# A hybrid decoder step: halved and woven products in the state-space stage, splits held behind its recurrences, later stores and delayed cache products

## The chip, the cores and the metric

The kernel runs on one core of a Trainium2 chip. The metric is the device time of one execution in microseconds, lower is better; the time before is the median of three runs.

## The reference

Two layers, D = 1024, 576 positions: a prompt of 512 and eight samples of 8. The first layer is attention over three groups of windows and dilations with a key/value cache, the second a diagonal complex state-space layer; a SwiGLU FFN (width 2816) follows each. Everything is fp32. The state-space layer, where most of the change lies:

```python
u = (h @ w_in).astype(f32)
abar = jnp.exp(lam * dt)                     # lam: complex, 64 groups x 64 states
bbar = ((abar - 1.0) / lam)[..., None] * bmat
# in chunks of time, state carried from one to the next:
bu = jnp.einsum('gpc,btgc->btgp', bbar, uk)
a_cum, x0 = lax.associative_scan(combine, (a_el, bu), axis=1)
xs = x0 + a_cum * hc[:, None]
y = jnp.einsum('gcp,btgp->btgc', cmat, xs).real   # + d_skip * u
g = jax.nn.gelu(y)
z = g @ w_glu
val, gate = jnp.split(z, 2, axis=-1)
return val * jax.nn.sigmoid(gate), h_last
```

The outputs are both results, the three shifted caches for prompt and samples, and the new states.

## The kernel before

Every large product is made of three: the weights and the activations are each split into a high part, rounded to the fp32r type, and a low rest, and high·high, low·high and high·low are summed in a PSUM bank. ScalarE makes the high part of a weight tile (`whi`, line 99) and VectorE the rest (`wlo`, line 100); `mm6` (line 108) issues the six products of a tile of 128 x 128 weights (two halves of 288 positions). Weights come in tiles of 512 KB on SP's DMA queue. `pace(rate)` adds the rate to a credit at each weight load and sends one store of the shifted cache (`o_kv_s`, line 83, about 1 MB) for each full unit; RF is the usual rate.

The stages follow each other: QKV projection in 36 steps j with the attention of cached samples woven in; attention of the prompt; output projection; FFN 0; the state-space layer; FFN 1. Instructions are put on each engine's queue by a scheduler that follows the order in which the code issues them and reorders what is ready.

In the QKV steps, `begin` handles the group of the longest cache: the tiles `kc` (keys) and `qb` (queries) are loaded one step ahead, and VectorE multiplies and reduces them (`P<-kc`). The list `due` holds the pairs of this step; `later(n, fn)` runs `fn` n slots on. VectorE also makes the norms of the projected rows (the five `sh<-t` reduces of a chunk), which the scores wait for. `kc` and `qb` share six buffers.

`ssm_setup` builds the constants of the state-space layer as a generator during FFN 0: after each half of a projection there, `fill` runs it to its next `yield`. We call this a tick. It makes E (powers of abar, on POOL), then for each of eight blocks f the matrices W, T and V, and stores all in DRAM. T comes from VectorE, V from POOL.

`ssm_phase` treats the width of 1024 as eight blocks f of 128 channels. `stage1(c)` projects two blocks (u = h w_in), stores the rows of u and loads them back in the layout of U. `stage2(f)` multiplies U by W into a PSUM bank (line 1423, 128 x 64 pieces), copies it to Sb (line 1425, ScalarE) and runs the recurrence over chunks on VectorE (lines 1438 to 1451): rotate by E, scan, rotate back, write Xt. `stage3(f)` adds T·U and V·Xt (lines 1461 and 1462), applies gelu (1464), stores the rows of y and loads them back, and splits them (lines 173 and 174) for the last product. `consts(f, q)` loads W, E, T and V of a block on queue q: blocks 0 to 3 during FFN 0, and block f + 4 behind `stage3(f)` on ScalarE's queue. There are three banks `acc` and one double bank `aux`. `glu_first` makes the first column of the GLU product: two banks for the gate (`pg`), two for the value (`pv`), over two halves of the contraction, rows of y 0 to 3 and 4 to 7.

## Time and profile before

| | us |
|---|---|
| median of 3 runs (1497.78 to 1498.53) | 1497.95 |
| profiled execution | 1499.43 |
| its span | 1497.7 |
| TensorE busy in the span | 1472.2 |
| VectorE busy | 895.8 |
| ScalarE busy | 527.8 |
| POOL busy | 323.1 |

A span is from the first to the last instruction; the profiled execution's time has 1.73 us around it. The granted TensorE clock was 0.998. A row of the timeline is start, duration, engine, line, operation, output<-input, tile form and shape, count, and in brackets the idle time of the engine before it with what released it. A row of the waits is engine, line, releaser: total, times, longest. A row of a stretch is its bounds and length, then busy time and instructions of PE, PE's weight loads, VectorE, ScalarE and POOL, then clock, DMA share and GB/s. A row of a DMA issue ends with KB and the median time to landing. SPq, ACTq and POOLq are the DMA queues of the engines.

### The profile page before, as it was taken

The page shows a single profiled execution, that of the slowest core. Times are in us where ns is not written, and L with a number is a line of the kernel's source. Part 1 is how long each engine was busy: PE and PEld are TensorE (multiplying, and loading weights), DVE is VectorE, ACT ScalarE, POOL GpSimd, SP SyncE. Part 2 cuts the span into 40 slices and gives each one's busy share as a digit, 9 for nine tenths or more (in the row PEclk, how much of TensorE's full clock was granted, in tenths as well). Part 3 has the DMA queues.
Part 4 walks back from the last instruction along what each step waited for, and adds up shares of the span by engine and source line. Part 5 has one row for each costly group of instructions (what it writes and reads, how often), then busy time and mean ns, then how long its engine had stood idle before and what let it go on. Part 6 is the DMA issues. An engine that isn't in the chain of part 4 may idle for free. (4 is left out here: it accounts for less than half of the span.)

```text
span 1497.7 us, 29564 instructions
## 1 busy us (share of the span) xinstructions
PE 1472.2 (98%) x12406; PEld 1384.5 (92%) x12406; DVE 895.8 (60%) x1507; ACT 527.8 (35%) x814; POOL 323.1 (22%) x377
## 2 busy tenths in 40 slices
PE   9999999999999999999999999999999999999998
PEld 7888777777899999999999999899999999999998
DVE  5898988745569545388687768745443323333332
ACT  4534455465552211322223453433432212221222
POOL 2022231320030174134436520201111001100100
PEclk9999999999999999999999999999999999999999
DMA  7566788989875555677867668865555655442212
GB/s 248 209 234 229 237 278 270 365 295 348 247 252 191 204 212 204 245 238 282 288 203 246 221 219 262 232 217 168 186 197 196 223 195 195 137 138 85 83 56 81
DMA packets 191861, 322.64 MB, mean 215 GB/s; under 512 B 40016, under 2 KB 138128, under 8 KB 190320
## 3 DMA queue, kind: packets, MB, share of 16 engines
q1 hardware_dynamic: 183488, 303.24, 60.0%
q10 hardware_dynamic: 5072, 10.04, 2.0%
q0 software_dynamic: 3168, 7.48, 1.5%
q8 instruction: 97, 1.59, 0.4%
q14 instruction: 36, 0.29, 0.1%
HBM read 289.22 MB, written 118.78 MB: 272 GB/s over the span
## 5 line engine op out<-in xcount | busy, mean ns | idle before, releaser
L108 PE MATMUL acc<-xgh,wlo 128*128 128x288 f32 x1760 | 377.9, 296 | 2.2 <-DVE wlo L100 2.2
L108 PE MATMUL acc<-xgh,whi 128*128 128x288 f32 x1760 | 379.1, 297 | 0.1
L108 PE MATMUL acc<-xgl,whi 128*128 128x288 f32 x1760 | 377.7, 296 | 1.0 <-DVE xgl L174 1.0
L100 DVE TENSOR_TENSOR wlo<-raw,whi 128x1024 fp32r<-128x1024 f32 (+1 forms) x166 | 214.9, 1295 | 261.9 <-ACT whi L99 258.4
L99 ACT ACTIVATE whi<-raw 128x1024 fp32r<-128x1024 f32 (+1 forms) x166 | 172.4, 1038 | 476.2 <-PE acc L108 446.0
L108 PEld LDWEIGHTS acc<-xgh,wlo 128*128 128x128 f32 x1760 | 283.2, 188 | 2.7 <-DVE wlo L100 2.5
L108 PEld LDWEIGHTS acc<-xgl,whi 128*128 128x128 f32 x1760 | 283.1, 189 | 1.5 <-DVE xgl L174 1.3
L108 PEld LDWEIGHTS acc<-xgh,whi 128*128 128x128 f32 x1760 | 282.7, 189 | 1.5 <-issue 1.0
L1029 POOL TENSOR_TENSOR gt<-gt,rstd 128x576 f32<-128x576 f32 x44 | 72.9, 1659 | 489.3 <-ACT gt L1028 489.1
L108 PE MATMUL acc<-hh,wlo 128*128 128x288 f32 x704 | 150.8, 295 | 2.1 <-DVE wlo L100 2.1
L108 PE MATMUL acc<-hh,whi 128*128 128x288 f32 x704 | 151.6, 296 | 0.0
L108 PE MATMUL acc<-hl,whi 128*128 128x288 f32 x704 | 150.9, 295 | 0.0
L340 PE MATMUL acc<-whi,xh 128*128 128x512 f32 x288 | 118.8, 414 | 0.5 <-ACT xh L280 0.4
L108 PEld LDWEIGHTS acc<-hh,wlo 128*128 128x128 f32 x704 | 112.9, 188 | 2.3 <-DVE wlo L100 2.3
L108 PEld LDWEIGHTS acc<-hh,whi 128*128 128x128 f32 x704 | 113.0, 188 | 0.6 <-issue 0.6
L108 PEld LDWEIGHTS acc<-hl,whi 128*128 128x128 f32 x704 | 113.1, 188 | 0.0
L340 PE MATMUL acc<-wlo,xh 128*128 128x512 f32 x288 | 112.2, 391 | 0.0
L340 PE MATMUL acc<-whi,xl 128*128 128x512 f32 x288 | 111.5, 393 | 0.0
L1050 DVE TENSOR_TENSOR xT<-acc,xT 128x576 f32<-128x576 f32 x48 | 36.1, 756 | 53.5 <-PE acc L108 53.5
L194 POOL TENSOR_TENSOR ssum<-ssum,sq 128x576 f32<-128x576 f32 x21 | 36.8, 1753 | 136.2 <-ACT sq L193 106.9
L340 PEld LDWEIGHTS acc<-whi,xl 128*128 128x128 f32 x288 | 54.0, 188 | 12.0
L340 PEld LDWEIGHTS acc<-whi,xh 128*128 128x128 f32 x288 | 54.0, 188 | 11.2 <-ACT xh L280 0.9
(395 smaller groups left out, 2008.5 us busy)
## 6 DMA issues: line engine op xcount, KB each, us to landing
o_kv_s<-cache_kv_w SPq DMA_DIRECT2D x64, 1020.0 KB, 6.9
kc<-cache_kv_w SPq DMA_DIRECT2D x100, 512.0 KB, 7.4
raw<-ffn_w_gate SPq DMA_DIRECT2D x44, 512.0 KB, 3.9
raw<-ffn_w_up SPq DMA_DIRECT2D x44, 512.0 KB, 3.9
raw<-ffn_w_down SPq DMA_DIRECT2D x40, 512.0 KB, 3.5
raw<-w_qkv SPq DMA_DIRECT2D x36, 512.0 KB, 7.4
kc<-qscr SPq DMA_DIRECT2D x32, 512.0 KB, 6.7
o_kv_s<-cache_kv_w SPq DMA_DIRECT2D x16, 1008.0 KB, 6.4
```

The costliest lines, as they stand in the source:

```text
L99: s.activation(hi, raw, AF.Copy)
L100: mark[0] = v.tensor_tensor(lo, raw, hi.bitcast(F32), OP.subtract)
L108: pem[0] = te.matmul(ps[:, c, :HN], w, x[:, c * HN:(c + 1) * HN], start=first and i == 0, stop=last and i == 2)
L194: g.tensor_tensor(self.ss, self.ss, sq, OP.add)
L340: ins = nc.tensor.matmul(*a, **kw)
L1029: g.tensor_tensor(t, t, nin.r, OP.mult)
L1050: v.tensor_tensor(xv, ps[m][:, :, :HN], xv, OP.add)
```

## The change

*State-space stage.* Each T and V product becomes two of 64 output columns. `stage1` takes a function `mid` that it runs inside its products: `stage2(1)` now stands before the last quarter of `stage1(2)`, `stage2(3)` and `stage3(0)` between the halves of `stage1(3)`. Constants of the second four blocks are loaded on POOL's queue: W and E behind `stage2(f)`, T and V behind `stage3(f)`. U has eight buffers, and the rows of y that come back use them too; u has two buffers of its own. The W products of blocks from 4 on alternate between two banks; Y of blocks 6 and 7 both use `aux`. The rows of y are split in two groups of four by `gsplit`, which holds the first group's splits behind Sb(7) on ScalarE and behind Xt(6) on VectorE, the second's behind the gelu of block 7 and Xt(7). `glu_first` puts `stage3(6)` and `stage3(7)` between its products and takes the second half of the contraction row by row.

*Setup.* Five yields fewer while E is made and two more between E's last copy and its store, so that what follows comes three ticks earlier; V's stores come one tick behind V's products.

*QKV steps.* In steps 8, 20, 24 and 28 the products of the cache are issued five slots later, and the closing of a sample 12 slots later instead of 10.

*Stores.* RF is 0.72 for 0.70, and the GLU weight loads send none (0.58 before).

```diff
-RF = 0.7
+RF = 0.72
...
+    def products(j, due):
+        for b, part, kc, qb in due:
+            if part == 0:
+                prods[b] = dk.tile([128, 4, 4, 8], F32, name="P2")
+                g.memset(prods[b], 0.0)
+            v.tensor_tensor(kc, kc, qb, OP.mult)
+            v.tensor_reduce(prods[b][:, :, 0:2, 2 * part:2 * part + 2].rearrange("p a h c -> p c a h"), kc.rearrange("p c (a h d) -> p c a h d", a=4, h=2),
+                            AX.X, OP.add)
+            if part == 3:
+                c = Close2(nc, L, v, s, dk, psd, "Sd", prods.pop(b), b)
+                later(12 if j <= 31 else 6, lambda c=c: close(c))
...
+        if due:
+            if j % 4 == 0 and j < 32 and CHUNKS[j // 4 - 1][0] < 2:
+                later(5, lambda: products(j, due))
+            else:
+                products(j, due)
...
-    def consts(f, q):
+    def consts_in(f, q):
         kc = kp[f // 2 % 2]
         Wc = kc.tile([128, 2, 4, 128], F32, name="Wc")
         q.dma_start(Wc, scn["W"][f])
         Ec = kc.tile([128, 2, 4, 64], F32, name="Ec")
         q.dma_start(Ec, scn["E"][f])
+        KC[f] = [Wc, Ec]
+
+    def consts_out(f, q):
+        kc = kp[f // 2 % 2]
         Tc = kc.tile([128, 8, 128], F32, name="Tc")
         q.dma_start(Tc, scn["T"][f])
         Vc = kc.tile([128, 4, 2, 128], F32, name="Vc")
         q.dma_start(Vc, scn["V"][f].rearrange("r p q l c -> (r p) q l c"))
-        KC[f] = (Wc, Vc, Tc, Ec)
-
-    out.update(Ar=Ar, Ai=Ai, E63=E63, rho=rho, x0=x0, xs0=xs0, KC=KC, consts=consts)
+        KC[f] += [Tc, Vc]
...
                 yield
-                yield
+                if k == 5:
+                    yield
             yield
             g.tensor_copy(E63, ee[:, :, :, 63])
+            yield
+            yield
             nc.sync.dma_start(scn["E"].rearrange("f p r q c -> p r f q c"), ee.rearrange("p r (f q) c -> p r f q c", f=8))
...
                 g.tensor_tensor(vv[:, 1], vv[:, 1], vt_, OP.subtract)
+                yield
                 for gl in range(2):
                     for ri in range(2):
                         nc.sync.dma_start(scn["V"][f, ri, :, :, gl, :], vv[gl * 64:gl * 64 + 64, ri].rearrange("p q c t -> p q (c t)"))
-                yield
...
+    pend, last = [], {}
+
+    def gsplit(n, a, b):
+        for f, yt in [pend.pop(0) for _ in range(n)]:
+            hi = xg.tile([128, NT], F32R, name="xgh")
+            lo = xg.tile([128, NT], F32R, name="xgl")
+            with tc.issue_after(last[a].ins):
+                s.activation(hi, yt, AF.Copy)
+            with tc.issue_after(last[b].ins):
+                v.tensor_tensor(lo, yt, hi.bitcast(F32), OP.subtract)
+            G[f] = hi, lo
...
-    def stage1(c):
+    def stage1(c, mid=None, at=(1, 0)):
...
             for m in range(2):
+                if mid and (kh, m) == at:
+                    mid()
...
-            u = wk.tile([128, 2, HN], F32, name="uP")
+            u = wk.tile([128, 2, HN], F32, name="yt", bufs=2)
...
-            U = wk.tile([128, 8, 72], F32, name="U", bufs=6)
+            U = wk.tile([128, 8, 72], F32, name="U", bufs=8)
...
-        S = acc(2)
+        S = acc(1 + f % 2 if f > 3 else 2 if f else 1)
...
         X[f] = Xt
+        if f < 4:
+            consts_in(f + 4, g)
...
-        Y = acc(0) if f % 2 else aux.tile([128, 2, 512], F32, name="aux")
+        U, (Tc, Vc) = Uc[f], KC[f][2:]
+        Y = acc(0) if f in (1, 3, 5) else aux.tile([128, 2, 512], F32, name="aux")
         for gl in range(2):
             for q in range(4):
-                o = Y[:, gl, q * 72:q * 72 + 72]
-                te.matmul(o, Tc[:, 2 * q + gl, :], U[:, 2 * q + gl, :], start=True, stop=False)
-                te.matmul(o, Vc[:, q, gl, :], X[f][:, gl, q, :], start=False, stop=True)
+                for w, x, st in ((Tc[:, 2 * q + gl, :], U[:, 2 * q + gl, :], True), (Vc[:, q, gl, :], X[f][:, gl, q, :], False)):
+                    for h in range(0, 128, 64):
+                        te.matmul(Y[h:h + 64, gl, q * 72:q * 72 + 72], w[:, h:h + 64], x, start=st, stop=not st)
...
-        yt = wk.tile([128, NT], F32, name="yt")
+        yt = wk.tile([128, 8, 72], F32, name="U", bufs=8).rearrange("p a b -> p (a b)")
         nc.sync.dma_start(yt, scn["Y"][f])
         if f < 4:
-            consts(f + 4, s)
-        G[f] = L["split"](xg, yt, None, "xgh", "xgl")
+            consts_out(f + 4, g)
+        pend.append((f, yt))
...
-        W2[c0] = [fetch_w(A["ssm_w_glu"], 2 * D, kh * 4, 4, c0, 256, 0.0 if c0 in (0, D) else 0.58) for kh in range(2)]
+        W2[c0] = [fetch_w(A["ssm_w_glu"], 2 * D, kh * 4, 4, c0, 256, 0.0) for kh in range(2)]
...
     stage2(0)
-    stage2(1)
-    stage1(2)
+    stage1(2, lambda: stage2(1), (1, 1))
     stage2(2)
-    stage2(3)
     fetch2(D)
-    stage1(3)
-    stage3(0)
+    stage1(3, lambda: (stage2(3), stage3(0)))
     stage3(1)
+    stage2(4)
     fetch2(0)
-    stage2(4)
+    stage3(2)
     stage2(5)
-    stage3(2)
     stage3(3)
     stage2(6)
     stage3(4)
     stage2(7)
-    for f in range(5, 8):
-        stage3(f)
-    sp["es"].close()
-    nout = L["Norm"](3, L["es"].enter_context(L["right"]("xg2", bufs=8)))
+    stage3(5)
+    gsplit(4, ("Sb", 7), ("Xt", 6))
...
     def glu_first():
-        pg, pv = [acc(1), acc(2)], [acc(0), aux.tile([128, 2, 512], F32, name="aux")]
-        for kh in range(2):
-            for ps, c0 in ((pg, D), (pv, 0)):
-                glu_half(ps, *split_w(W2[c0][kh]), kh)
+        pg = [acc(1), acc(2)]
+        glu_half(pg, *split_w(W2[D][0]), 0)
+        stage3(6)
+        wh, wl = split_w(W2[0][0])
+        pv = []
+        for m in range(2):
+            pv.append(aux.tile([128, 2, 512], F32, name="aux") if m else acc(0))
+            for k in range(4):
+                mm6(pv[m], wh[:, k, m * 128:(m + 1) * 128], wl[:, k, m * 128:(m + 1) * 128], *G[k], k == 0, False)
+            if m == 0:
+                stage3(7)
+        gsplit(4, ("ys", 7), ("Xt", 7))
+        sp["es"].close()
+        N[0] = L["Norm"](3, L["es"].enter_context(L["right"]("xg2", bufs=8)))
+        w = [(ps, *split_w(W2[c0][1])) for ps, c0 in ((pg, D), (pv, 0))]
+        for k in range(4):
+            for ps, wh, wl in w:
+                for m in range(2):
+                    mm6(ps[m], wh[:, k, m * 128:(m + 1) * 128], wl[:, k, m * 128:(m + 1) * 128], *G[4 + k], False, k == 3)
         return pg, pv
```

The order on TensorE around block 0 of stage 3 (L108 are products of the input projection of the last two blocks). Before, at the end of that projection:

```order
L108 MATMUL acc_10837<-xgh,whi 128x288 x2
L108 MATMUL acc_10837<-xgl,whi 128x288 x2
L108 MATMUL acc_10837<-xgh,wlo 128x288 x2
L1461 MATMUL aux<-U,Tc 128x72
L1462 MATMUL aux<-Xt,Vc 128x72
```

After, between its halves:

```order
L108 MATMUL acc_10806<-xgh,whi 128x288 x2
L108 MATMUL acc_10806<-xgl,whi 128x288 x2
L108 MATMUL acc_10806<-xgh,wlo 128x288 x2
L1454 MATMUL acc_10863<-U,Wc 64x72 x16
L1495 MATMUL aux<-U,Tc 64x72 x2
L1495 MATMUL aux<-Xt,Vc 64x72 x2
```

Block 0 now stands half a projection earlier, with the W products of block 3 (L1454) ahead of it, and T and V (both L1495) come in pairs of halves of 64 columns.

The order on VectorE at the end of the recurrences: the splits of the rows of y are L174 before and L1417 after. Before, block 7 from its first sums to its end:

```order
L1440 TENSOR_TENSOR R<-R,ta 128x256
L1441 TENSOR_TENSOR R<-R,ta 128x256
L174 TENSOR_TENSOR xgl<-yt,xgh 128x576
L1443 SCALAR_TENSOR_TENSOR Z<-tb,R 128x256 x2
L1446 TENSOR_TENSOR R<-Ec,Z 128x8x63
L1447 TENSOR_TENSOR ta<-Ec,Z 128x8x63
L174 TENSOR_TENSOR xgl<-yt,xgh 128x576
L1450 TENSOR_TENSOR Xt<-R,ta 64x4x63
L1451 TENSOR_TENSOR Xt<-R,ta 64x4x63
L1450 TENSOR_TENSOR Xt<-R,ta 64x4x63
L1451 TENSOR_TENSOR Xt<-R,ta 64x4x63
L174 TENSOR_TENSOR xgl<-yt,xgh 128x576 x4
```

After, from the end of block 6's recurrence (its last rows L1481 and L1482):

```order
L1481 TENSOR_TENSOR Xt<-R,ta 64x4x63
L1482 TENSOR_TENSOR Xt<-R,ta 64x4x63
L1417 TENSOR_TENSOR xgl<-U,xgh 128x576 x2
L1469 TENSOR_TENSOR R<-Ec,Sb 128x512
L1470 TENSOR_TENSOR ta<-Ec,Sb 128x512
L1417 TENSOR_TENSOR xgl<-U,xgh 128x576
L1471 TENSOR_TENSOR R<-R,ta 128x256
L1472 TENSOR_TENSOR R<-R,ta 128x256
L1474 SCALAR_TENSOR_TENSOR Z<-tb,R 128x256 x2
L1477 TENSOR_TENSOR R<-Ec,Z 128x8x63
L1478 TENSOR_TENSOR ta<-Ec,Z 128x8x63
L1417 TENSOR_TENSOR xgl<-U,xgh 128x576
```

The rows of y that were split inside the recurrences as they came now stand behind Xt of block 6, two of them ahead of block 7 and two inside it.

The order on VectorE in QKV step 24, where a product of the cache (`kc<-kc`, with its reduce `P<-kc`) meets the norm's reduces (`sh<-t`; `Sall` belongs to the scores). Before:

```order
L760 TENSOR_TENSOR wlo<-raw,whi 128x1024
L760 TENSOR_TENSOR kc<-kc 128x1024
L760 TENSOR_REDUCE P_1726<-kc 128x2x4x2
L760 TENSOR_REDUCE sh<-t_1887 128x8
L760 TENSOR_REDUCE sh<-t_1903 128x8
L760 TENSOR_REDUCE sh<-t_1928 128x8
L760 TENSOR_REDUCE sh<-t_1944 128x8
L760 ISA Sall,mx_77<-Sall,md 128x136
L760 ISA mx_77 128x1
L760 TENSOR_REDUCE sh<-t_1965 64x8
L760 TENSOR_TENSOR wlo<-raw,whi 128x1024
```

After:

```order
L767 TENSOR_TENSOR wlo<-raw,whi 128x1024
L767 TENSOR_REDUCE sh<-t_1885 128x8
L767 TENSOR_REDUCE sh<-t_1901 128x8
L767 TENSOR_REDUCE sh<-t_1926 128x8
L767 TENSOR_REDUCE sh<-t_1942 128x8
L767 ISA Sall,mx_77<-Sall,md 128x136
L767 ISA mx_77 128x1
L767 TENSOR_REDUCE sh<-t_1963 64x8
L767 TENSOR_TENSOR kc<-kc 128x1024
L767 TENSOR_REDUCE P_1726<-kc 128x2x4x2
L767 TENSOR_TENSOR wlo<-raw,whi 128x1024
```

The product and its reduce moved from ahead of the five reduces to behind them.

32 lines of the change are left out of this document (13 added, 19 removed).

## The prediction

> **What bounds the kernel now.** I read the page's engine table first, then the waits of TensorE, then busy time by stretch, and last the timeline of each engine where TensorE waits.
>
> ```profile
> PE 1472.2 (98%) x12406; PEld 1384.5 (92%) x12406; DVE 895.8 (60%) x1507; ACT 527.8 (35%) x814; POOL 323.1 (22%) x377
> PE acc L108 <- DVE wlo L100: 4.3, 2, 2.2
> PE Sd L578 <- ACT ks L760: 2.2, 2, 1.6
> 896.74:990.63 93.89, 90.67 (x895) 88.36 (x894) 70.64 (x119) 39.18 (x87) 11.27 (x19) 1.00 0.81 246
> ```
>
> TensorE is busy for 98% of the span, so a change can win in two ways only: less matrix work, or one of the short waits gone (engine line, releaser, us in total, times, longest). The last row is the state-space stage from the end of its second input projection to the end of the first output product: 93.89 us, of which TensorE is idle 3.2. Yet VectorE has a hole of 6.5 us in that stage:
>
> ```profile
> 905.12 0.69 DVE L1438 TENSOR_TENSOR R<-Ec,Sb 128x512 f32<-128x512 f32 x1
> ...
> 939.10 0.69 DVE L1438 TENSOR_TENSOR R<-Ec,Sb 128x512 f32<-128x512 f32 x1 [6.49 <-ACT Sb L1425]
> ...
> 945.60 0.69 DVE L1438 TENSOR_TENSOR R<-Ec,Sb 128x512 f32<-128x512 f32 x1
> ...
> 952.71 0.75 DVE L174 TENSOR_TENSOR xgl<-yt,xgh 128x576 fp32r<-128x576 f32 x1
> ...
> 958.79 0.42 DVE L1451 TENSOR_TENSOR Xt<-R,ta 64x252 f32<-64x252 f32 x1
> ```
>
> A recurrence (L1438 to L1451) takes 6.50 us (939.10 to 945.60). The fifth, of block 4, waits for ScalarE's Sb copy; the seventh has a split of a row of y inside it and ends at 959.21. The last GLU products follow that chain.
>
> ```profile
> 936.54 0.65 ACT L1464 ACTIVATE ys<-acc 128x576 f32<-128x576 f32 x1 [3.23 <-DMA u_scr<-uP]
> 938.44 0.63 ACT L1425 ACTIVATE Sb<-acc 128x576 f32<-128x576 f32 x1
> 925.03 0.57 SPq L83 DMA_DIRECT2D o_kv_s<-cache_kv_w  x1
> 926.44 2.18 SPq L1409 DMA_DIRECT2D u_scr<-uP  x2
> 936.11 0.37 SPq L1413 DMA_DIRECT2D U<-u_scr  x1
> 990.63 0.42 PE L108 MATMUL acc<-xgh,whi 128*128 128x288 f32 x2
> ```
>
> ScalarE came to the Sb copy late, behind the second gelu, which was itself held for 3.23 us, and SP sent a 1 MB cache store just ahead of the rows of u, whose loads left 9.7 us after the stores. The first product of the next GLU column starts at 990.63: the stage's end.
>
> **Halved T and V products.** Now and after:
>
> ```profile
> 930.69 0.39 PE L1461 MATMUL acc<-U,Tc 128*128 128x72 f32 x2
> ...
> 934.04 0.39 PE L1462 MATMUL acc<-Xt,Vc 128*128 128x72 f32 x2
> 934.35 1.22 PE L1423 MATMUL acc<-U,Wc 128*64 128x72 f32 x32
> 935.50 0.44 PE L1461 MATMUL aux<-U,Tc 128*128 128x72 f32 x2
> ```
>
> One block's T and V products are 32 records of 128*128, in 16 rows of two; the last starts 15 rows after the first (930.69 to 934.04), 0.223 us each, so a block takes 3.57 us. The W products already have the form that the change gives them, 128*64 with 72 columns: 32 records from 934.35 to 935.50, 1.15 us. The change makes 64 such records of a block, 2.30 us. It saves 1.27 us a block, 10.2 us over eight. Going from one form to the other costs 0.31 − 0.22 = 0.09 us (934.04 to 934.35, against 0.22 between like rows); the finer weave adds some six such borders, 0.6 us. [...] The W row bears out 3.57 / 2.30 = 1.55x, and I take that.
>
> **The weave.** I rebuild the stage from 896.74, the start of the stretch above, where both kernels start block 0's W products, with 0.1325 us for a projection product (four from 926.37 to 926.90):
>
> ```profile
> 926.37 0.42 PE L108 MATMUL acc<-xgh,whi 128*128 128x288 f32 x2
> 926.63 0.43 PE L108 MATMUL acc<-xgl,whi 128*128 128x288 f32 x2
> 926.90 0.42 PE L108 MATMUL acc<-xgh,wlo 128*128 128x288 f32 x2
> 909.44 0.73 DVE L1408 TENSOR_TENSOR uP<-acc,rs_m 128x576 f32<-128x576 f32 x1
> 581.87 1.23 DVE L100 TENSOR_TENSOR wlo<-raw,whi 128x1024 fp32r<-128x1024 f32 x1
> ```
>
> TensorE up to block 4's W products: 192 projection products (25.4), five W groups (5.8), blocks 0 and 1 of stage 3 (4.6), a wait for u of block 6 that clears the bank (some 1.3) and borders (0.3): 896.74 + 37.4 = 934.15; with ScalarE's 0.65 the fifth recurrence can start at 934.9. VectorE: block 1's W products now stand three quarters into the third projection and end near 908.6, so its recurrence starts at 909.4 instead of 905.12, a cost of 4.3 us that the old hole pays for. From there three recurrences (19.5), four rows of u (3.0), two weight splits (2.4) end at 934.3. The two engines meet within a microsecond: block 4 starts at 934.95, 4.15 earlier than 939.10. Blocks 4, 5 and 6 run without a split inside: 934.95 + 19.5 = 954.4 for the end of Xt(6), against 959.21. Behind it VectorE does two splits, block 7 and two more splits: 954.4 + 1.4 + 6.5 + 1.4 = 963.7.
>
> TensorE waits for that end, since V(6) needs it. What then follows without a break: stage 3 of block 6 (2.2), 72 products (9.5), stage 3 of block 7 (2.3, at 966.1, its Xt ready at 963.7), the gelu that clears the one aux bank (0.9), 120 products (15.9), borders (0.5): 31.3 us, ending at 985.7. Before, 990.63 − 959.21 = 31.4. So this stage gains 4.9 us: of 10.2 us of matrix work, half goes into new waits of TensorE for Xt(5) and Xt(6), some 3 us each, in place of the old ones.
>
> What hides the moved loads. The constants go to POOL's queue, in order behind waits for the recurrences; T and V of block 4 leave once block 2's recurrence is done (near 925) and are used at 941.5.
>
> ```profile
> Tc<-t_scr ACTq DMA_DIRECT2D x4, 512.0 KB, 6.4
> o_kv_p<-vt POOLq DMA_DIRECT2D x8, 256.0 KB, 6.8
> ```
>
> Landing in 6 to 7 us leaves several to spare; later blocks too. The rows of u of block 6 leave at 931.4, without the cache store; even at the old 9.7 us plus landing, W(6) at 947 just makes the recurrence at 947.95. The held splits: the last row of y is stored at 969 and needed after 980. I put all of this at nothing; without the cover it is the second rival.
>
> **First FFN, setup in fewer ticks.**
>
> ```profile
> 850.95 0.53 PE L108 MATMUL acc<-hh,wlo 128*128 128x288 f32 x2 [2.10 <-DVE wlo L100]
> 848.47 2.43 DVE L100 TENSOR_TENSOR wlo<-raw,whi 128x1024 fp32r<-128x1024 f32 x1
> 847.34 2.48 POOL L194 TENSOR_TENSOR ssum<-ssum,sq 128x576 f32<-128x576 f32 x1
> 596.56 0.53 PE L108 MATMUL acc<-xgh,wlo 128*128 128x288 f32 x2 [2.24 <-DVE wlo L100]
> 587.72 0.31 DVE L1298 MEMSET cb<- 128x128 f32 x2 [4.62 <-DMA e_scr<-ee]
> ```
>
> At 848.47 a weight split takes 2.43 us instead of 1.23 beside POOL, which is doing the last V products and sums of the norm together. Three ticks fewer put the V products before the down projection, so I count this wait gone: −2.1 (0 if the sums alone slow VectorE). [...] At 587.72 VectorE stood behind the E table's store; the store now leaves two ticks after its copy. Between 0 and −2.2, and a setup that has moved by three ticks against the gate loop can meet a weight split anew, +1 to +2: I take −1.
>
> **Delayed products of the cache.**
>
> ```profile
> 194.24 1.23 DVE L760 TENSOR_TENSOR kc<-kc 128x1024 f32<-128x1024 f32 x1 [3.53 <-DMA kc<-qscr]
> 195.50 1.22 DVE L760 TENSOR_REDUCE P<-kc 128x16 f32<-128x1024 f32 x1
> 198.51 0.43 PE L578 MATMUL Sd<-ks,Qz 128*32 128x128 f32 x8 [1.63 <-ACT ks L760]
> PE pt L566 <- DMA kc<-cache_kv_w: 1.3, 1, 1.3
> ```
>
> The 2.2 us at L578 are two waits, this one and a like one of 0.57, the rest of the sum. The norm's reduces, whose results the scores wait for, were queued behind a product that waits for its DMA; product and reduce are 2.45 us, more than either wait, and now stand behind them. −2.2 then; but the buffers come free later, and a cache tile late as in the last row costs 1.3 each, at most two: +2.6 less 2.2. I take −1.
>
> **The rest.** The store pace only moves transfers; FFN 2's tail of stores still ends ahead of the last products. Zero.
>
> **Sum.** −4.9 − 2.1 − 1 − 1 = −9.0 on the profiled 1499.43 (span 1497.7 and 1.73 around it), 1490.4; the median of the runs is 1.48 below the profiled one, so **1489.0**. No change means within 0.2%, 3.0 us.
>
> **The rivals.** *The recurrences do not hold TensorE.* Then all 10.2 us and the 3.2 idle go, less 0.6 of borders: −12.8 in the stage, 1481.1. For it: VectorE is busy only 70.64 of 93.89. Against: four recurrences in a row are 26 us and cannot start before block 4's W products. 0.10.
> *The hole stays.* Rows of u or Sb(4) come late again, block 4 starts near 939 and the end of Xt(6) at 959: the stage gains nothing, the rest −4.1, 1493.9; with the FFN and cache terms failing too, 1498. For it: block 1 starts 4.3 us later, and POOL holds the loads in order. 0.20.
> *Constants one at a time, slower.* If POOL's eight T and V transfers from 925.7 are served one after another, at 5.0 us each Vc(7) lands at 966, just in time; at 7.5 at 985.7, 19.7 late, and the stage ends at 1005.4, +14.8: 1508.6 with the other terms. Slower than before from 6.2 us each on (9 us late). For it: 6.4 to 6.8 us a landing above, with 0.81 of the DMA engines busy over the stage (its row, the number before the last). Against: median landings of loads that may have overlapped say nothing of one-at-a-time service. 0.07. [...]
> *The products stay one behind another.* If halves did not overlap, a block would take 64 records of 0.11, 7.1 us, and lose; the W row excludes it.
>
> **How the numbers follow.** Forecast 0.58 (1486 to 1493), the hole 0.20, free recurrences 0.10, slow constants 0.07, else 0.05. The range 1482 to 1497.5 takes in the first, most of the hole and half of the free case. Faster 0.80 (0.58 + 0.10 + half of the hole + 0.02), same 0.12, slower 0.08.
>
> **What would show it.** T and V rows of 128*64 with 2.3 us a block; VectorE from 909 to 934 without a hole; block 4 at 935; Xt(6) at 954; TensorE idle about 3 us before V(5) and V(6); no 2.10 wait near 850 and no 1.63 near 198. I am wrong if block 4 starts after 938, or a wait for Tc, Vc or Ec by DMA shows.

## The result and the profile after

The changed kernel takes 1489.44 us (median of 5, 1488.16 to 1493.70), the kernel before 1498.53 (median of 5) on the same chip: a ratio of 0.9938, 95% interval 0.9922 to 0.9955. One of the five runs of before stands apart at 1752.71; the others lie from 1497.78 to 1499.42. The profiled execution took 1488.62 with a span of 1486.7, so the profiled time of after is 10.8 us below that of before, and its span 11.0. The forecast was 1489.0. The sum came out; its terms did not, and the experiments are about them.

First the page's engine line and TensorE's own waits after the change (us in total, times, longest):

```profile
PE 1457.7 (98%) x12662; PEld 1370.9 (92%) x12662; DVE 896.0 (60%) x1507; ACT 526.8 (35%) x814; POOL 335.4 (23%) x393
...
PE acc L1454 <- DMA U<-u_scr: 9.3, 1, 9.3
...
PE acc L108 <- DVE wlo L100: 1.9, 2, 1.7
...
PE pt L573 <- DMA kc<-cache_kv_w: 1.4, 2, 1.1
```

TensorE is busy 14.5 us less (1472.2 to 1457.7) and the weight splits cost it 1.9 instead of 4.3. The 2.2 us of the scores are gone. In their place stands one wait of 9.3 us that the prediction did not have: the W products of a block (L1454) for the rows of u.

To see where the 11.0 us come from, compare the same landmarks in both timelines of TensorE: the first scores of the prompt, the first product of FFN 0, block 0's W products. Before:

```profile
304.78 0.66 PE L760 MATMUL S<-kT,att 64*32 64x256 f32 x16
424.14 0.42 PE L108 MATMUL acc<-xgh,whi 128*128 128x288 f32 x2
896.74 1.22 PE L1423 MATMUL acc<-U,Wc 128*64 128x72 f32 x32
```

After, with the first product of the next GLU column, which ends the stage:

```profile
301.29 0.66 PE L767 MATMUL S<-kT,att 64*32 64x256 f32 x16
419.96 0.43 PE L108 MATMUL acc<-xgh,whi 128*128 128x288 f32 x2
887.94 1.22 PE L1454 MATMUL acc<-U,Wc 128*64 128x72 f32 x32
979.65 0.43 PE L108 MATMUL acc<-xgh,whi 128*128 128x288 f32 x2
```

The QKV steps gain 3.5 us (forecast 1), the attention 0.7 (forecast 0), FFN 0 4.6 (472.60 to 467.98; forecast 3.1), so 8.8 us are won before the state-space stage. The stage, of which 4.9 were forecast, goes from 93.89 to 91.71 and gives 2.2:

```profile
887.94:979.65 91.71, 80.44 (x1153) 77.78 (x1153) 68.32 (x117) 38.19 (x86) 19.14 (x35) 0.94 0.72 214
```

TensorE works 10.2 us less there (90.67 to 80.44), but is idle 11.3 instead of 3.2.

**The halved products.** Block 0's T and V products are 16 rows of four; the first and the last:

```profile
912.14 0.29 PE L1495 MATMUL aux<-U,Tc 128*64 128x72 f32 x4
...
914.01 0.29 PE L1495 MATMUL aux<-Xt,Vc 128*64 128x72 f32 x4
```

Fifteen rows in 1.87 us are 0.125 a row, 2.00 us a block, against 3.57 before: 1.79 times as fast, and better than the 2.30 taken from the W products. Over eight blocks 12.6 us of matrix work go.

**The recurrences.** VectorE, the first instruction of blocks 1, 4, 5 and 6 and the last of block 6, in brackets how long VectorE stood idle ahead of it:

```profile
900.84 0.69 DVE L1469 TENSOR_TENSOR R<-Ec,Sb 128x512 f32<-128x512 f32 x1 [1.15 <-ACT Sb L1456]
...
925.99 0.69 DVE L1469 TENSOR_TENSOR R<-Ec,Sb 128x512 f32<-128x512 f32 x1 [0.93 <-ACT Sb L1456]
...
932.49 0.69 DVE L1469 TENSOR_TENSOR R<-Ec,Sb 128x512 f32<-128x512 f32 x1
...
942.96 0.69 DVE L1469 TENSOR_TENSOR R<-Ec,Sb 128x512 f32<-128x512 f32 x1 [4.07 <-ACT Sb L1456]
...
948.99 0.42 DVE L1482 TENSOR_TENSOR Xt<-R,ta 64x252 f32<-64x252 f32 x1
```

Block 4 starts 38.05 us after block 0's W products; forecast 38.2 (934.95 − 896.74), before 42.4. Of the old hole of 6.49 us 0.93 is left. Then a new one opens two blocks later: block 6 waits 4.07 us, for this:

```profile
940.00 2.19 PE L1454 MATMUL acc<-U,Wc 128*64 128x72 f32 x32 [9.31 <-DMA U<-u_scr]
```

The rows of u of block 6 were stored at 921.55, and their load was issued at 927.25 (SP's queue); it landed 12.6 us later. POOL sent the T and V constants of block 6 at the same moment, those of block 7 behind them; those of block 5 had left at 923.98. The issues on SP, those on POOL, and the landing times of the loads into U (rows of u, and rows of y that come back):

```profile
921.55 0.34 SPq L1440 DMA_DIRECT2D u_scr<-yt  x1
...
927.25 0.64 SPq L1444 DMA_DIRECT2D U<-u_scr  x1
```
```profile
927.00 0.53 POOL L1111 DMA_DIRECT2D Tc<-t_scr  x1 [1.85 <-PE aux L1495]
927.52 0.53 POOL L1113 DMA_DIRECT2D Vc<-v_scr  x1
...
930.87 0.53 POOL L1111 DMA_DIRECT2D Tc<-t_scr  x1 [2.70 <-DMA u_scr<-yt]
931.38 0.53 POOL L1113 DMA_DIRECT2D Vc<-v_scr  x1
```
```profile
DMA to landing us min/median/max: 2.6/3.9/12.6
```

And by stretch: PE is at zero, the DMA engines (the number before the last) are all busy, and the granted clock (before it) falls to half:

```profile
932.00:936.00 4.00, 0.00 (x0) 0.00 (x0) 3.84 (x8) 0.00 (x0) 0.03 (x1) 0.56 1.06 392
936.00:940.00 4.00, 0.00 (x0) 0.03 (x1) 2.73 (x6) 0.00 (x0) 0.00 (x0) 0.50 1.16 322
940.00:944.00 4.00, 4.00 (x86) 4.00 (x88) 1.04 (x2) 2.53 (x9) 0.00 (x0) 0.66 0.85 209
```

So the W products of block 6 took 2.19 us where they take 1.22 at the full clock, and the recurrence started later by that too. That is the price of a wait twice over.

### The profile page after: what moved, and what is told of

Same layout as the page of the kernel before. It is cut to its first block, busy times and chain, and to the rows that moved or that the text cites. A ratio compares the mean times of both kernels' runs of the same rounds, so it can differ in the third digit from the quotient of the medians.

```text
span 1486.7 us, 30078 instructions
## 1 busy us (share of the span) xinstructions
PE 1457.7 (98%) x12662; PEld 1370.9 (92%) x12662; DVE 896.0 (60%) x1507; ACT 526.8 (35%) x814; POOL 335.4 (23%) x393
## 4 chain that ended last, share of the span: by engine, by line
PE 85%; DVE 4%; DMA 4%; POOL 3%; issue 2%; ACT 2%; SPq 0%; ACTq 0%; DVEq 0%; POOLq 0%
PE acc L108 62%; PE acc L340 12%; PE Sd L767 2%; DMA kc<-cache_kv_w 1%; PE S L767 1%; PE O L767 1%; PE pt L573 1%; DMA U<-u_scr 1%; PE aux L108 1%; PE pt L767 1%; DVE u L767 1%; PE aux L1495 1%; DMA y_scr<-ys 1%; DMA e_scr<-ee 1%; DVE a L767 1%
## 5 line engine op out<-in xcount | busy, mean ns | idle before, releaser
L108 PE MATMUL acc<-xgh,whi 128*128 128x288 f32 x1760 | 379.5, 297 | 0.1
L108 PE MATMUL acc<-xgh,wlo 128*128 128x288 f32 x1760 | 375.9, 295 | 1.9 <-DVE wlo L100 1.9
L108 PE MATMUL acc<-xgl,whi 128*128 128x288 f32 x1760 | 377.5, 295 | 0.0
L100 DVE TENSOR_TENSOR wlo<-raw,whi 128x1024 fp32r<-128x1024 f32 (+1 forms) x166 | 209.2, 1260 | 232.6 <-ACT whi L99 229.1
L108 PEld LDWEIGHTS acc<-xgh,wlo 128*128 128x128 f32 x1760 | 282.6, 188 | 2.5 <-DVE wlo L100 2.3
L108 PEld LDWEIGHTS acc<-xgh,whi 128*128 128x128 f32 x1760 | 281.7, 188 | 2.1 <-issue 1.2
L108 PEld LDWEIGHTS acc<-xgl,whi 128*128 128x128 f32 x1760 | 282.6, 188 | 0.2
L1036 POOL TENSOR_TENSOR gt<-gt,rstd 128x576 f32<-128x576 f32 x44 | 76.7, 1744 | 486.6 <-ACT gt L1035 486.4
L108 PE MATMUL acc<-hh,whi 128*128 128x288 f32 x704 | 151.3, 296 | 0.0
L108 PE MATMUL acc<-hh,wlo 128*128 128x288 f32 x704 | 150.6, 295 | 0.0
L108 PE MATMUL acc<-hl,whi 128*128 128x288 f32 x704 | 150.6, 295 | 0.0
L340 PE MATMUL acc<-whi,xh 128*128 128x512 f32 x288 | 118.7, 414 | 2.0 <-ACT xh L280 1.8
L108 PEld LDWEIGHTS acc<-hh,whi 128*128 128x128 f32 x704 | 112.9, 188 | 0.4 <-issue 0.4
L108 PEld LDWEIGHTS acc<-hl,whi 128*128 128x128 f32 x704 | 113.0, 188 | 0.0
L108 PEld LDWEIGHTS acc<-hh,wlo 128*128 128x128 f32 x704 | 112.9, 188 | 0.0
L340 PE MATMUL acc<-wlo,xh 128*128 128x512 f32 x288 | 112.2, 391 | 0.0
L340 PE MATMUL acc<-whi,xl 128*128 128x512 f32 x288 | 111.5, 393 | 0.0
L1035 ACT ACTIVATE gt<-gt 128x576 f32<-128x576 f32 x44 | 30.1, 685 | 100.7 <-DVE gt L1034 100.6
L340 PEld LDWEIGHTS acc<-whi,xh 128*128 128x128 f32 x288 | 54.0, 188 | 12.6 <-ACT xh L280 2.4
```

Source lines behind the costliest of these rows:

```text
L100: mark[0] = v.tensor_tensor(lo, raw, hi.bitcast(F32), OP.subtract)
L108: pem[0] = te.matmul(ps[:, c, :HN], w, x[:, c * HN:(c + 1) * HN], start=first and i == 0, stop=last and i == 2)
L340: ins = nc.tensor.matmul(*a, **kw)
L1035: s.activation(t, t, AF.Silu)
L1036: g.tensor_tensor(t, t, nin.r, OP.mult)
```

## The experiments

The theory after this profile: the constants of blocks 6 and 7 share the DMA engines with the rows of u of block 6, which is what ate the stage's gain. The rival: something else on that path is late (the store of u, SP's queue, the bank), and T and V are bystanders. For the terms ahead of the stage: delayed products, fewer ticks and store rate each did what the prediction gave them, or the gain comes from elsewhere or from luck. All kernels are the changed one with the edit shown, unless it says otherwise. The table is from each kernel's profiled execution, whose single runs differ; the medians and intervals stand with each experiment. Columns: start of the prompt's scores, FFN 0 to block 0's W products, the stage from there to the next GLU column, and the wait for the rows of u of block 6.

| kernel | scores | FFN 0 | stage | wait for u |
|---|---|---|---|---|
| before | 304.78 | 472.60 | 93.89 | none |
| after | 301.29 | 467.98 | 91.71 | 9.31 |
| again | 302.40 | 467.89 | 92.56 | 9.53 |
| hold_tv67 | 302.00 | 467.88 | 87.14 | 4.40 |
| hold_tv7 | 302.10 | 467.84 | 91.32 | 6.74 |
| no_late_tv | 302.38 | 467.88 | 87.48 | 0.98 |
| full_tv | 302.26 | 467.64 | 99.50 | none |
| act_queue | 302.86 | 467.87 | 91.71 | 4.89 |
| hold_tv567 | 301.79 | 468.02 | 95.87 | 3.84 |
| products_back | 302.31 | 467.84 | 93.52 | 10.32 |
| yields_back | 305.39 | 470.87 | 91.25 | 9.72 |
| rate_070 | 302.50 | 469.84 | 91.59 | 9.40 |
| before_halved | 305.04 | 471.22 | 92.05 | none |
| outer_alone | 301.98 | 468.40 | 96.99 | none |

**The changed kernel again** (no edit), on the chip of hold_tv67, no_late_tv and full_tv.

> The changed kernel itself, as the measure for the runs beside it on the same chip. Both theories: 1488 to 1491 us, and TensorE waits at the W products of block 6 for the rows of u (9.3 us in the profile shown); if that wait is an accident of one run it is below 3 us here.

1492.55 us (8 runs, 1490.43 to 1494.31), ratio 0.9962 [0.9949, 0.9975], against 1498.55 for before. The same kernel is 3 us above the first measurement and above the 1488 to 1491 expected; its wait, now 9.53 us, is there again. In the profiled run of this second measurement the clock was at half for two stretches, one of them in the attention:

```profile
378.90:385.70 6.80, 6.58 (x84) 5.07 (x84) 3.20 (x12) 2.94 (x9) 0.00 (x0) 0.50 0.62 202
```

6.8 us at half the clock with TensorE busy for 6.58 cost some 3 us (3.3 if the work goes at half its speed). The attention is 3.6 us longer than in the first profile.

**T and V of blocks 6 and 7 held back.**

```diff
-        if f < 4:
+        if f < 2:
             consts_out(f + 4, g)
...
     stage2(6)
+    with tc.issue_after(last["Sb", 6].ins):
+        consts_out(6, s)
     stage3(4)
     stage2(7)
+    with tc.issue_after(last["Sb", 7].ins):
+        consts_out(7, s)
     stage3(5)
```

> T and V of blocks 6 and 7 are loaded on ScalarE's queue behind Sb(6) and Sb(7), so 2 MB of loads leave after the rows of u of block 6 have landed and not beside them. Contention theory (the constants' loads fill the 16 DMA engines just when the rows of u are loaded back): the wait of 9.3 us at the W products of block 6 falls below 5, block 6's recurrence starts 2 to 4 us earlier, 1485 to 1487.5 us. Order theory (the rows of u are late because SP's queue sends the rows of y, a store and a weight tile ahead of them): the wait stays above 8, 1488 to 1491.

1487.28 (6 runs), ratio 0.9929 [0.9914, 0.9944]: 5.3 us less than the changed kernel beside it. TensorE, VectorE and the loads of U:

```profile
935.61 2.19 PE L1454 MATMUL acc<-U,Wc 128*64 128x72 f32 x32 [4.40 <-DMA U<-u_scr]
```
```profile
933.87 0.69 DVE L1469 TENSOR_TENSOR R<-Ec,Sb 128x512 f32<-128x512 f32 x1
940.37 0.69 DVE L1469 TENSOR_TENSOR R<-Ec,Sb 128x512 f32<-128x512 f32 x1
```
```profile
DMA to landing us min/median/max: 2.8/4.3/7.4
```

The slowest landing falls from 12.6 to 7.4, block 6 follows block 5 without a hole (6.50 apart), and the stage takes 87.14 us, 1.8 less than the 88.96 that the prediction built (985.7 − 896.74). This version beats both kernels.

**T and V of blocks 4 to 7 not loaded**: the blocks use those of 0 to 3, so 4 MB of constants and the right values of these blocks are left out.

```diff
         if f < 4:
-            consts_out(f + 4, g)
+            KC[f + 4] += KC[f][2:]
```

> T and V of blocks 4 to 7 are not loaded at all; those blocks use T and V of blocks 0 to 3 instead. 4 MB less between 914 and 932 us. Contention theory: the rows of u of block 6 land within 5 us of their load's issue, the wait at the W products of block 6 is below 2 us, the six-hundredths of clock lost there return too, 1484 to 1486 us. Order theory: the wait stays above 7, 1488 to 1491.

1487.48 (6 runs), ratio 0.9932 [0.9915, 0.9949]. The wait is down to 0.98, yet the time is that of holding two blocks and above the 1484 to 1486 expected, since the next thing is late:

```profile
935.50 1.22 PE L1454 MATMUL acc<-U,Wc 128*64 128x72 f32 x32 [0.98 <-DMA U<-u_scr]
...
940.16 0.51 PE L1495 MATMUL aux<-U,Tc 128*64 128x72 f32 x4 [2.27 <-ACT ys L1497]
```

The single double bank `aux` is cleared by the gelu, and with the loads out of the way TensorE waits there. So with the work in this order the late loads of T and V cost some 5 us (1492.55 to 1487.48).

**T and V of block 7 alone held back**: of the edit of hold_tv67 the part for block 7, with `f < 3`.

> The changed kernel with only T and V of block 7 held behind Sb of block 7, on ScalarE's queue; T and V of block 6 stay on POOL's queue behind block 2. If the wait for the rows of u of block 6 is a matter of the bytes in flight, it shrinks by about half of what holding both blocks took off it (9.3 to 4.4): 6.5 to 7.5, and the time lies between the changed kernel and that one, 1489 to 1491. Rival (the constants of block 6 are the ones in flight with these rows, those of block 7 come behind them): the wait stays near 9 and the time at the changed kernel's, 1491 to 1492.5.

1490.21 (4 runs), ratio 0.993 [0.9907, 0.9952].

```profile
938.76 2.19 PE L1454 MATMUL acc<-U,Wc 128*64 128x72 f32 x32 [6.74 <-DMA U<-u_scr]
```

With the pairs of T and V taken out one after another the wait is 9.31, 6.74 (without 7), 4.40 (without 6 and 7): 2.57 and 2.34 us for each megabyte. One megabyte at the 392 GB/s of the stretch 932 to 936 takes 2.7 us. So it is the bytes, and not one of the two pairs, that make the load late. The stage, however, gained only 0.4 us in this trace: from Xt(6) to its end 32.1 us pass (948.20 to 980.33) instead of 30.2, with TensorE busy 31.11 instead of 29.45, because products that ran ahead of Xt(6) now stand behind it: from the W products of block 6 to the end of Xt(6) TensorE issued 198 products instead of 225, with a new wait of 1.02 for a split of y and a clock of 0.80 instead of 0.86.

**The late constants on ScalarE's queue** (W, E, T and V of blocks 4 to 7):

```diff
-            consts_in(f + 4, g)
+            consts_in(f + 4, s)
...
-            consts_out(f + 4, g)
+            consts_out(f + 4, s)
```

> The changed kernel with all late constants on ScalarE's queue, W and E behind stage 2 and T and V behind stage 3 as in the change. Same bytes at about the same time. Contention theory: the rows of u of block 6 still land late, TensorE waits 5 us or more at its W products or at ScalarE's copies behind the loads; 1488 to 1493. Rival (POOL's queue as such makes the loads slow or starves others): that wait falls below 3 us, 1485 to 1487.

1491.93 (6 runs), ratio 0.996 [0.9944, 0.9976]: as the changed kernel. In its trace the wait halves, and another takes up what it gave:

```profile
936.82 2.00 PE L1454 MATMUL acc<-U,Wc 128*64 128x72 f32 x32 [4.89 <-DMA U<-u_scr]
...
946.17 0.35 PE L1495 MATMUL acc<-U,Tc 128*64 128x72 f32 x4 [2.85 <-ACT ys L1497]
```

ScalarE's own timeline says what held that gelu: a store of y, which had not landed.

```profile
945.47 0.65 ACT L1497 ACTIVATE ys<-acc 128x576 f32<-128x576 f32 x1 [5.92 <-DMA y_scr<-ys]
```

Another queue does not make the bytes fewer. In this run only the small transfer that came late changed: now the store of y (5.92), and less the rows of u (4.89 instead of 9.31).

**T and V of blocks 5, 6 and 7 held back**, each behind its Sb, with `f < 1`.

> T and V of blocks 5, 6 and 7 on ScalarE's queue behind Sb(5), Sb(6), Sb(7). Contention theory: 1 MB less beside the rows of u than with two blocks held; the wait at the W products of block 6 falls from 4.4 to below 2.5 us and the halved clock may stay away: 1484 to 1487. If another wait (T and V of block 5 now late, or three splits ahead of block 7) takes its place: 1486 to 1489.

1492.69 (8 runs), ratio 0.9953 [0.9933, 0.9973]. A miss: the wait for u shrank by 0.56 only, to 3.84, and the stage became 95.87. For the first the times give a likely reason: in this kernel T and V of block 5 left at 929.93, just behind the load of u (928.22), so the edit moved their megabyte and did not take it away.

TensorE has a new wait of 6.97 for a gelu (releaser L1497), and ScalarE shows what stood ahead of that gelu: a split that waited for its row of y to come back.

```profile
951.15 0.85 PE L108 MATMUL acc<-xgh,whi 128*128 128x288 f32 x2 [6.97 <-ACT ys L1497]
```
```profile
949.88 0.68 ACT L1415 ACTIVATE xgh<-U 128x576 fp32r<-128x576 f32 x1 [5.97 <-DMA U<-y_scr]
```

T and V of blocks 6 and 7 left at 938.0 and 941.5 in this kernel, when that row was on its way. It is the same delay with another victim; that the constants caused this one too is read from the times and was not tried apart.

**T and V at 128 columns again**, the weave kept: the two products of before in the place of the four.

> T and V products at the full 128 columns, all else as in the changed kernel. A block then takes 3.57 us and not 2.00. If the recurrences and the rows of u set the pace (my theory), only the two blocks behind Xt(6) cost their 1.6 us each and the first two are absorbed by the wait for the rows of u: plus 3 to 4, 1491 to 1494. If TensorE set the pace, all eight cost: plus 12.6, 1501.

1497.65 (12 runs, 1490.20 to 1501.28), ratio 0.9984 [0.9964, 1.0004]. The runs fall into two groups that the mean granted clock tells apart: four at 0.999 to 1.000 with 1490.2 to 1493.4 us, eight at 0.992 to 0.995 with 1497.1 to 1501.3. The profiled run is of the second group. There is no wait for u (TensorE comes to block 6 at 937.0, when the rows are there), but a short one for a bank, and behind it a stretch at half the clock with TensorE fully busy:

```profile
945.04 0.44 PE L1494 MATMUL acc<-U,Tc 128*128 128x72 f32 x2 [1.97 <-ACT ys L1496]
```
```profile
947.00:960.80 13.80, 13.80 (x65) 13.80 (x65) 13.30 (x26) 5.55 (x15) 2.26 (x5) 0.51 0.54 143
```

13.8 us at half the clock are 6.2 to 6.8 us lost: rows of two products take 0.48 us instead of 0.265 there (597.81 to 598.29 in the profile of before), which is 45% of the stretch, and half of it at the most. Taken out, the stage of 99.50 is 92.7 to 93.3. The changed kernel had TensorE busy at a clock of 0.66 for the 4 us from 940, which cost some 1.4, so its stage would be 90.3, and its profiled run 1487.3 where the four runs at the full clock, on another chip, begin at 1490.2. The full products thus cost some 3 us, the theory's size, and not the rival's 12.6; the rest of their work stands where the changed kernel waits for u. The median of 1497.65 is outside the 1491 to 1494 of the theory, and the lower clock of eight of the twelve runs goes with that.

**The kernel before with halved T and V products alone.**

```diff
-                te.matmul(o, Tc[:, 2 * q + gl, :], U[:, 2 * q + gl, :], start=True, stop=False)
-                te.matmul(o, Vc[:, q, gl, :], X[f][:, gl, q, :], start=False, stop=True)
+                for w, x, st in ((Tc[:, 2 * q + gl, :], U[:, 2 * q + gl, :], True), (Vc[:, q, gl, :], X[f][:, gl, q, :], False)):
+                    for h in range(0, 128, 64):
+                        te.matmul(Y[h:h + 64, gl, q * 72:q * 72 + 72], w[:, h:h + 64], x, start=st, stop=not st)
```

> The kernel before with one edit, the T and V products in halves of 64 columns. Rows of the changed kernel give 2.00 us a block instead of 3.57, so 12.6 us of matrix work go over eight blocks. Theory (the stage is held by the chain of copies and recurrences, and shorter products only help where they stand behind it): the recurrences start as before (block 4 near 939, Xt of block 6 done near 959), only the blocks behind Xt(6) gain, 2 x 1.57 = 3.1, so the end comes 3 us earlier, 1495.4, with the idle time of TensorE in the stage some 9 us larger. Rival (TensorE itself holds the stage): all of it goes, the end 11 to 12.6 earlier, 1486 to 1487.5. Should the granted clock be halved for one or more stretches of 3.4 us behind the new waits, each costs up to 1.7 us.

1497.12 (12 runs), before 1499.11, ratio 0.9981 [0.9969, 0.9994]: 2 us of the 12.6. On VectorE block 4 starts when it did, behind the same hole, and TensorE has new waits:

```profile
939.06 0.69 DVE L1438 TENSOR_TENSOR R<-Ec,Sb 128x512 f32<-128x512 f32 x1 [6.38 <-ACT Sb L1425]
```
```profile
939.08 2.19 PE L1423 MATMUL acc<-U,Wc 128*64 128x72 f32 x32 [1.97 <-ACT Sb L1425]
...
948.89 0.35 PE L1462 MATMUL aux<-U,Tc 128*64 128x72 f32 x4 [1.95 <-ACT ys L1464]
```

In this trace TensorE is idle for 9.35 us of the stage instead of 3.2, and two stretches of 3.4 us at half the clock (from 938.5 and from 949; a mean of 0.74 over 936 to 942 and of 0.51 over 949 to 952.5) cost it some 3 more. So with less to do for TensorE, here the copies, gelus and recurrences hold the stage, and most of the saved work turns into waits and into what the clock takes behind them.

**The kernel before with the changed QKV steps, ticks and store rate alone.** The edits are those of the change, outside the state-space stage, whose GLU loads still send stores.

> The kernel before with the changed QKV steps, the ticks of the setup and the store rate of 0.72 alone; the state-space stage stays as before (its GLU loads still send stores at 0.58). Theory (the two parts are independent): W products of block 0 start near 888 instead of 896.7, the stage then lasts as before, so the gain is the 8.8 us before it in the profile, of which some 2 us were luck of the clock: 1490 to 1492. Rival (stage and outer part trade transfers, a store more or less in the stage): the rows of u of block 4 or 6 land later or earlier and the stage itself is over 2 us longer or shorter. By the prediction's terms it would be -4.1, 1494.4.

1498.08 (12 runs, 1494.88 to 1507.14), ratio 0.9995 [0.9978, 1.0011]. Also a miss: the profiled run reaches the stage 6.8 us earlier than before (889.98), and the stage then takes 96.99, 3.1 more.

```profile
934.47 1.22 PE L1433 MATMUL acc<-U,Wc 128*64 128x72 f32 x32 [2.60 <-ACT Sb L1435]
```
```profile
936.00:940.00 4.00, 4.00 (x22) 4.00 (x21) 3.84 (x8) 2.11 (x8) 0.11 (x1) 0.52 1.05 261
940.00:946.00 6.00, 6.00 (x51) 5.73 (x50) 5.71 (x11) 2.24 (x8) 0.11 (x1) 0.50 1.10 331
```

A wait of 2.60 for Sb(4), then 10 us at half the clock with TensorE fully busy, some 5 us lost; without them the stage would take 92, 2 less than before. So in this profile the gain ahead of the stage is there, and the clock takes it back in the stage. Which of the twelve runs had which stretches cannot be seen, since only one is profiled; their mean clocks go from 0.996 (1494.9) to 0.990 (1507.1), with a median of 0.994 against 0.998 for the runs of before.

**The products of the cache as before** (no delay, the closing 10 slots later).

> The changed kernel with the cache products of the QKV steps where they stood before (closings after 10 slots). My theory: the waits at the scores near 198 and 238 us (1.63 and 0.57) return and the wait for a cache tile near 278 (1.1) goes; the attention starts 2 to 3.5 us later; 1492 to 1495 if the changed kernel stands at 1490 to 1492. Rival (the 3.5 us gained by step 28 come from elsewhere, the loads and not the order): no wait at L578's line, attention within 0.7 us of the changed kernel's.

1494.0 (12 runs, 1490.51 to 1502.38), ratio 0.9973 [0.9955, 0.9991], too wide to price an edit of 1 us. The trace is clearer: the scores start at 302.31, and of TensorE's waits in the QKV steps 0.98 at L582 (the scores) and 0.65 are left, 1.63 us; before it was 4.1 (0.63, 1.28, 1.63 and 0.57). So the expected 1.63 and 0.57 at the scores came back as one wait of 0.98 only, and the scores start 2.5 us ahead of before without the new order.

**The ticks as before.**

> The changed kernel with the setup's yields of before. My theory: the waits for a weight split near 592 (above 2.0 and perhaps with the clock halved for one 3.4 us stretch) and near 846 (2.1) return: FFN 0 is 2.5 to 4.5 us longer, 1493 to 1496. Rival (the setup's alignment does not matter, the long splits come from POOL's sums of the norm alone): a wait near 846 stays away or is below 0.5, FFN 0 within 1 us.

1494.16 (12 runs), ratio 0.9968 [0.9955, 0.9982], 1.6 above the changed kernel's second measurement, which ran on another chip. FFN 0 is 3.0 us longer, and waits for splits are back near 850, not as one of 2.10 but as two for the low parts (and one of 0.43 for a high part):

```profile
848.33 0.54 PE L108 MATMUL acc<-hh,wlo 128*128 128x288 f32 x2 [0.91 <-DVE wlo L100]
...
859.72 0.54 PE L108 MATMUL acc<-hh,wlo 128*128 128x288 f32 x2 [0.84 <-DVE wlo L100]
```

The wait near 596 stays at 1.70, so it is not the ticks that shortened it. The later scores (305.39) are not the ticks', which come after them: this run had 3.4 us at half the clock near its start (a product of L340 every 0.43 us from 11.5 to 14.8, and every 0.23 behind it) and a wait of 1.44 for a cache tile.

**The store rate as before**, RF 0.70.

> The changed kernel with one number put back: the store rate RF 0.70 for 0.72. The prediction put the rate at zero. Theory (the rate only moves transfers): the first FFN stays at 467.9 us from its first product to block 0's W products, the wait at its weight split near 592 stays at 1.70, the time within 1 us of the changed kernel's, 1490 to 1492.5. Rival (the rate places a cache store beside that weight split or beside the cache tiles of the QKV steps): the wait is 2.24 again and the granted clock halves behind it, or the prompt's attention starts some 3 us later; +2 to +4, 1492 to 1496.

1491.94 (5 runs), before 1499.7, ratio 0.9943 [0.9929, 0.9956]. In the median nothing shows; in the trace the rival holds: the wait near 596 is back with half a clock behind it, and FFN 0 is 1.9 us longer.

```profile
594.86 0.53 PE L108 MATMUL acc<-xgh,wlo 128*128 128x288 f32 x2 [2.31 <-DVE wlo L100]
```
```profile
595.90:599.30 3.40, 3.40 (x17) 3.40 (x16) 2.31 (x4) 1.74 (x3) 0.98 (x1) 0.50 1.24 461
```

The scores start at 302.50, with the delayed products and the old rate; without the delay and with the new rate it was 302.31; with neither 304.8 and 305.0, with both 301.3 to 302.9 (yields_back aside).

## Why the prediction came out

**The halved products: right, and larger than taken.** 2.00 us a block, not 2.30. That much of the saved work would go into waits is shown from both sides: before_halved turns 12.6 us of work into 2, and full_tv at the full clock gives back only 3.

**The weave: right to block 5, wrong at block 6.** Block 4 came 38.05 us after block 0's W products where 38.2 was forecast. The step that failed is the one that put the moved loads "at nothing": "even at the old 9.7 us plus landing, W(6) at 947 just makes the recurrence at 947.95". The time from store to load was even shorter, 5.7 us; it was the landing, 12.6 us. I had asked whether the constants arrive in time for their own products, and they did: no wait for Tc, Vc or Ec is in the trace, and block 4 started in time, so neither of the signs that I had named for being wrong showed. What the constants push back while in flight is the small load on another queue: 9.31 us of wait for the rows of u with them, 0.98 without T and V of blocks 4 to 7 (no_late_tv). W(6) started 52.1 us after block 0's W products, 1.8 later than the 947 of the forecast; at half the clock it took 1.0 more, and the forecast's margin had been short by the other 1.0. So Xt(6) ended after 61.5 us instead of 57.7, 3.8 late; behind it the stage ran 30.2 us instead of 31.3, in part since T and V were faster (0.3 a block). Together 2.7: the gain of 2.2 instead of 4.9. The waits also stand elsewhere than forecast: some 3 us each before V(5) and V(6) are not in the trace, and all but 2 us of TensorE's idle time in the stage is the one wait at W(6). Behind it TensorE is busy for 38.57 of the 39.65 us to the end (the forecast had 38.7 from 947 to 985.7), so in that part TensorE itself sets the pace. That the mechanism is contention is shown by hold_tv7, hold_tv67 and no_late_tv, whose waits are 6.74, 4.40 and 0.98; act_queue, with 4.89 and 5.92, shows that it does not need POOL's queue. The rival of slow constants named the right resource and the wrong victim.

**FFN 0, the wait at 850: right.** −2.1 forecast, the wait is gone; with the ticks put back the waits return, in another shape, and FFN 0 is 3.0 us longer.

**FFN 0, the wait at 596: the cause was wrong, and part of the gain is luck.** I took −1 from the E table's later store. The wait went from 2.24 to 1.70, and in addition the half clock that followed it is gone. Before, TensorE's rows of two products behind the wait, the first and the ninth:

```profile
597.45 0.56 PE L108 MATMUL acc<-xgh,wlo 128*128 128x288 f32 x2
...
601.10 0.42 PE L108 MATMUL acc<-xgl,whi 128*128 128x288 f32 x2
```

Eight rows in 3.65 us, instead of 2.12 at 0.265 each, cost 1.5 us, which I had not priced. With the 0.54 it is −2.1. The wait goes with the store rate and not with the ticks: it is 2.24, 2.25 and 2.31 in the three profiles at 0.70 and 1.60 to 1.74 in the eleven at 0.72, yields_back among these. The half clock behind it does not go with the rate. In before and rate_070 it follows the wait; before_halved, whose FFN 0 is that of before, has the same wait and keeps the full clock (the number before the last two):

```profile
598.78 0.53 PE L108 MATMUL acc<-xgh,wlo 128*128 128x288 f32 x2 [2.25 <-DVE wlo L100]
```
```profile
592.00:602.00 10.00, 7.75 (x59) 7.51 (x58) 9.86 (x14) 0.49 (x1) 0.38 (x1) 1.00 0.69 244
```

Its FFN 0 takes 471.22, 1.4 less than that of before. So of the 4.6 us won in FFN 0 some 1.4 are the luck of the one profiled run, and from 471.22 to 467.98 the edits give 3.2, where 3.1 was forecast.

**The cache products: the sign right, the size open.** −1 forecast, −3.5 in this profile, 1.9 to 3.0 in the others that have the whole edit of these steps (against 304.78, yields_back with its early half clock aside). The waits at the scores near 198 and 238 went as forecast, and the one near 189 shrank from 1.28 to 0.32, for a new one of 1.08 at the cache tile:

```profile
277.98 0.55 PE L573 MATMUL pt<-ident,kc 128*128 128x128 f32 x3 [1.08 <-DMA kc<-cache_kv_w]
```

That one was in the working (1.3 each). The store rate alone (products_back) and the delay alone (rate_070) reach the scores 2.5 and 2.3 us earlier, and both together little more. These differences are against one profile of before, though. before_halved has the same QKV steps, no wait near 189, and 3.4 us at half the clock behind 198 (its products at L340 and L566 take some 1.7 us longer in total than in before); without these some 1.5 us it would be at the scores at 303.5, only 0.6 to 2.2 us behind the kernels with the whole edit. What follows the edits in every profile are the two waits at the scores: 1.63 and 0.57, 1.66 and 0.60 without them, none with the delay, one of 0.98 with the rate alone. So the forecast of −1 is not refuted, and the −3.5 is not the edits' alone. "The store pace only moves transfers … Zero" is the other step that failed: at 596 and at the scores a moved transfer is a moved wait.

**The sum.** The terms outside the stage gave 8.8 instead of 4.1, the stage 2.2 instead of 4.9: two errors of opposite sign. Of the 4.7 us too much outside, some 1.4 are the half clock in the profile of before and 0.7 the attention, where nothing was changed. With the stretches at half the clock taken out on both sides, the kernels with all the outer edits reach block 0's W products 5 to 8 us ahead of before and before_halved (at 888 to 890 instead of 895 to 896), still more than 4.1. The second measurement (1492.55) shows how much of the agreement to half a microsecond is chance: the same kernel came out 3 us higher on another chip.

What stays open is what decides whether a wait is followed by half a clock, and what share of the QKV gain each of its two causes has in the median. An earlier load of u of block 6 was not tried, and neither were the later splits, the banks and the stores left out of the GLU loads one by one.

## What to carry to other kernels

When loads are moved, ask not only whether they come in time for their users, but which small load on the critical path will be in flight with them, and hold the large ones behind the step that this small one feeds, as hold_tv67 did; then ask what they meet there, since hold_tv567 lost by it. Where a chain on other engines holds a stage, as in before_halved, faster matrix work turns into waits (2 us won of 12.6), and a wait can cost again by the clock behind it, as the 2.60 us in outer_alone, with some 5 us lost behind it. Test the terms of a sum one by one, since two kernels that differ by the sum of five edits can agree with it by two errors.

## What the hardware showed that was not expected

The granted clock of TensorE went to one half in these runs for stretches of 3.4 us (rate_070, from 595.9), 6.8 and 10.2 (again, from 378.9 and 938.7) and 13.8 (full_tv, from 947.0, at a mean of 0.51). They begin within some 2 us of the end of a wait, or inside a long one: behind 1.97 us (full_tv), 2.31 (rate_070), 2.60 (outer_alone), and in the attention (again), where TensorE stood idle for 1.70 of the 4 us from 376, but not behind 2.10 (before, near 851) or another 1.70 (after, near 592). The wait at the weight split near 596 had it behind it at 2.24 (before) and 2.31 (rate_070) and not at 2.25 (before_halved). In twelve runs of one kernel (full_tv) the mean clock parts the times into two groups with medians of 1490.8 and 1498.8.

A load of 288 KB of rows took 12.6 us to land with the DMA engines fully busy (a share of 1.06 and 1.16 from 932 to 940), where the median of the loads into U is 3.9, and each of the two megabytes of blocks 6 and 7 beside it cost the wait 2.3 to 2.6 us, close to the 2.7 us that a megabyte takes at the 392 GB/s of that stretch.
